# A batched matmul with a subtraction: the first row tile as a segment of its own, and the weight in two contiguous halves

## The chip, the cores and the metric

The kernel runs on one core of one Trainium2 chip. The metric is the device time of one execution, in microseconds (us). Beside it stands a profile of one execution: its span runs from the first to the last instruction, and its device time is a little longer than its span.

## The reference

```python
batch, m, k, n = 16, 512, 1024, 768
def reference(x, weight, sub_value):
    return (np.matmul(x, weight) - sub_value).astype(np.float32)
```

`x` is 16x512x1024, `weight` 1024x768, `sub_value` and the output 16x512x768, all in float32. With the batch flattened this is one matmul of 8192 rows. It reads 33.6 MB of `x`, 3.1 MB of `weight` and 25.2 MB of `sub_value`, and writes 25.2 MB.

## The kernel before, in words

The 8192 rows are cut into 64 row tiles of 128 ("tile 0" to "tile 63"). A tile's work runs through all engines:

1. SyncE (SP) issues the transfers, in the order of the list `TRANSFERS` (L29 to L36). An entry is a kind (x, w, s for `sub_value`, o for output), a first tile and a number of tiles: `('x', 3, 3)` brings tiles 3 to 5 of `x`. A transfer is issued by `issue()` (L243) and waits on SP for what it overwrites or sends: an x transfer for the casts of the tiles whose ring places it takes (16 places, `x_ring`), an s transfer for the outputs that leave the 32 places of `so_ring`, an o transfer for the subtractions. SP does this in order, so a transfer that waits holds up all behind it.
2. ScalarE (ACT) casts a tile to float16 (`cast`, L306, instruction L324). The cast also permutes k, so that pairs of float16 can be transposed as one 32-bit word, and so that a transposed chunk meets the rows of `weight` that sit on the same partitions.
3. TensorE (PE) transposes the tile with four 128x128 matmuls against an identity into PSUM (`transposes`, L342), and ACT copies the result to SBUF (L355, "the evacuation"). For nine pairs of tiles (`ON_DVE`: 10 and 11, 16 and 17, and so on) VectorE (DVE) transposes instead (L375). The casts of these pairs come seven tiles ahead of their use, those of other tiles four ahead.
4. PE multiplies: four chunks c, in each of them two weight loads (L404) and four matmuls of 128x384 (L199), into one of three PSUM accumulators (`po_b`, `NPO = 3`).
5. DVE subtracts (`finish`, L424): it reads the accumulator and the place of `so_ring` that holds `sub_value`, and writes the result in that place. The accumulator is free after that.

Which rows are a tile is set by `SEGMENTS` (L14) and `view` (L127). Rows are grouped in segments of 8 tiles, 1024 rows; in a segment partition p holds 8 consecutive rows, and tile j of the segment takes row j of each partition. So one tile's `x` comes as 128 pieces of 4 KB that lie 32 KB apart in DRAM, and a transfer of n tiles as 128 pieces of n times 4 KB.

The weight is read in the same manner (`w_rows`, L134): partition p holds rows 8p to 8p+7, and each of the two transfers `('w', 0, 2)` and `('w', 2, 2)` takes half of these rows, so 128 pieces of 12 KB, 24 KB apart. DVE casts each half in four instructions (L269).

The head is written out by hand (L445 to L488). `idle(n)` (L433) puts one weight load and n matmuls on zeros into PE's queue, whose result is not used. The first three tiles (`HEAD = 3`) go chunk by chunk, as `weight` arrives in halves. On PE the order is: 14 idle matmuls; transposes of tile 0; 7 idle; tile 0 chunk 0; 1 idle; tile 0 chunk 1; 2 idle; transposes of tiles 1 and 2; 1 idle; chunks 0 and 1 of tiles 1 and 2; chunk 2 of tiles 0, 1, 2; chunk 3 of tiles 0, 1, 2, each followed on DVE by its subtraction; transposes of tiles 3 and 4; tile 3, with the transposes of tile 5 in between. On ACT the casts of tiles 3 and 4 are followed by the evacuations of 3 and 4, then the cast of 5 and its evacuation. From tile 4 on a regular order follows (L492), and from there PE's instructions stand in a loop of six tiles per turn.

The wait that ties PE to the subtractions is in `matmuls`: chunk 0 of a tile takes the accumulator that the tile three before it had, and waits for that tile's `finish` (L397). The one that ties it to ACT is the wait for the tile's evacuation (L393).

Of the kernel before, what the change touches and what calls it, by code (L numbers as in the profile page):

```python
# [8 lines left out]
P = 128  # L9
# [1 line left out]
F32 = mybir.dt.float32  # L11
F16 = mybir.dt.float16

SEGMENTS = [(at, 8) for at in range(0, 64, 8)]  # L14
NX, NSO = 16, 32
N16, NXT, NPT, NPO = 4, 4, 2, 3
N16P, NXTP = 2, 1
# [6 lines left out]
HEAD = 3  # L24
# [2 lines left out]
LOOP = (4, 6, 10)  # L27

TRANSFERS = [  # L29
# [75 lines left out]
def kernel(  # L105
# [7 lines left out]
    nc = tc.nc  # L113
# [10 lines left out]
    n_c = KW // P  # L124
# [6 lines left out]
        rows = flat[first * P : (first + size) * P].rearrange("(p j) c -> p j c", p=P, j=size)  # L131
        return rows[:, at - first : at - first + n]

    w_rows = weight.rearrange("(p k) n -> p k n", p=P)  # L134

    section = ctx.enter_context(ExitStack())
    section.enter_context(tc.tile_critical(no_gpsimd_drain=True))  # L137
# [13 lines left out]
    x_ring = sbuf("x_ring", [P, NX, K], F32)  # L151
# [21 lines left out]
    sp, pe = Queue(nc, nc.sync), Queue(nc, nc.tensor)  # L173
# [69 lines left out]
    def issue():  # L243
        nonlocal known, from_w
        while todo:
            kind, at, n = todo[0]
            span = set(range(at, at + n))
            old = {t - NX if kind == "x" else t - NSO for t in span}
            need, by = {
                "w": (set(), "o"),  # L250
                "x": ({t for t in old if t >= 0}, "cast"),
                "s": ({t for t in old if t >= 0}, "o"),
                "o": (span, "finish"),
            }[kind]
            if not need <= done[by]:
                return
            todo.pop(0)
            done[kind] |= span
            if kind == "w":

                first = NSO - 2 * (n_c - at)
                st = so_ring[:, first : first + 2 * n]
                sem, value = lane((kind, at))
                sp.add(lambda st=st, at=at, n=n: nc.sync.dma_start(out=st, in_=w_rows[:, 2 * at : 2 * (at + n)]), then=(sem, 16))  # L264
                for c in range(at, at + n):
                    for r in range(2):
                        here = so_ring[:, first + 2 * (c - at) + r]
                        dve.add(
                            lambda c=c, r=r, here=here: nc.vector.tensor_copy(out=w_sb[:, c, r], in_=here),  # L269
                            waits=[(sem, value)], then=count("w"),  # L270
                        )
                        staged[first + 2 * (c - at) + r] = so_far["w"]
                    w_at[c] = so_far["w"]
                from_w |= {(("w", at), so_far["w"])}
                continue
            ring, size, flat = {
                "x": (x_ring, NX, x_flat), "s": (so_ring, NSO, sub_flat), "o": (so_ring, NSO, out_flat)
            }[kind]
            here = ring[:, at % size : at % size + n]
            there = view(flat, at, n)  # L280
            waits = []
            if kind == "x" and need:
                waits.append((counter["cast"], max(cast_at[t] for t in need)))
                last = max(need, key=lambda t: cast_at[t])
                known |= {tag for t, tag in of_x.items() if t in cast_at and cast_at[t] <= cast_at[last]}
            if kind == "s":
                for t in need:
                    waits.append(landed["o", t])
                    known.add(of_o[t])
                for t in span:  # L290
                    if t % NSO in staged:
                        waits.append((counter["w"], staged.pop(t % NSO)))
                        known |= {tag for tag, value in from_w if value <= waits[-1][1]}
            if kind == "o":
                waits.append((touched, 16))
                waits.append((counter["finish"], max(finish_at[t] for t in need)))
                known |= {of_s[t] for t in finish_at if finish_at[t] <= max(finish_at[u] for u in need)}
            sem, value = lane((kind, at))
            for t in span:
                landed[kind, t] = (sem, value)  # L300
                {"x": of_x, "s": of_s, "o": of_o}[kind][t] = (kind, at)
            if kind == "o":
                here, there = there, here
            sp.add(lambda here=here, there=there: nc.sync.dma_start(out=here, in_=there), waits, (sem, 16))  # L304

    def cast(mi):  # L306
        assert mi in done["x"]
        done["cast"].add(mi)
        x_in = x_ring[:, mi % NX].rearrange("p (q c r) -> p c q r", c=n_c, r=2)
        first = mi - mi % 2  # L310
        waits = [landed["x", mi]]
        if first in ON_DVE:
            if mi == first:
                b, before = take("x16p", N16P, mi)
                if before is not None:
                    waits.append((counter["pair"], pair_at[before]))
            to = x16p_b[:, slot["x16p", first], mi - first]
        else:
            b, before = take("x16", N16, mi)
            if before is not None:  # L320
                waits.append((counter["turn"], turn_at[before]))
            to = x16_b[:, b]
        to = to.rearrange("p (c q r) -> p c q r", c=n_c, r=2)
        act.add(lambda: nc.scalar.copy(out=to, in_=x_in), waits, count("cast"))  # L324
        cast_at[mi] = so_far["cast"]
        issue()
# [57 lines left out]
    def matmuls(mi, c):  # L384
        first = mi - mi % 2
        on_dve = first in ON_DVE or first == EARLY
        waits = []
        if c == 0:
            b, before = take("po", NPO, mi)
            if on_dve:  # L390
                waits.append((counter["pair"], pair_at[first]))
            if not on_dve:
                waits.append((counter["evac"], evac_at[mi]))  # L393
            elif mi == first:
                waits.append((counter["evac"], evac_at[mi + 1 if mi == EARLY else mi - 1]))
            if before is not None:
                waits.append((counter["finish"], finish_at[before]))  # L397
        if mi < HEAD:
            waits.append((counter["w"], w_at[c]))
        xt = xtp_b[:, slot["xtp", first], mi - first] if on_dve else xt_b[:, slot["xt", mi]]  # L400
        po = po_b[:, slot["po", mi]]
        for r in range(2):
            weights = xt[:, 2 * P * c + r : 2 * P * (c + 1) : 2]
            pe.add(lambda weights=weights: nc.tensor.ldweights(weights, tile_position=(0, 0)), [w for w in waits if w[0] in ready])  # L404
            waits = [w for w in waits if w[0] not in ready]
            for h in range(2):
                last = c == n_c - 1 and r == 1 and h == 1
                pe.add(lambda r=r, h=h, weights=weights: loaded_matmul(
                    po[:, h, :NS],
                    weights,  # L410
                    w_sb[:, c, r, h * NS : (h + 1) * NS],
                    start=(c == 0 and r == 0),
                    stop=(c == n_c - 1 and r == 1),
                ), waits, count("mul") if last else None)
                waits = []
        if c == n_c - 1:
            mul_at[mi] = so_far["mul"]

    def finish(mi):
# [8 lines left out]
        issue()  # L428

    issue()  # L430


    def idle(n):  # L433
        pe.add(lambda: nc.tensor.ldweights(idle_w, tile_position=(0, 0)), [(counter["idle"], 2)])  # L434
        for _ in range(n):
            pe.add(lambda: loaded_matmul(po_b[:, NPO - 1, 0], idle_w, idle_x, start=True, stop=True))
# [4 lines left out]
    def transpose_tile(mi):  # L441
        for f in transposes(mi):
            f()
# [4 lines left out]
    transpose_tile(0)  # L448
    idle(7)
    matmuls(0, 0)  # L450
    idle(1)
    matmuls(0, 1)
    idle(2)
    cast(1)
    cast(2)
    transpose_tile(1)
    transpose_tile(2)
    idle(1)
    for mi in (1, 2):
        for c in (0, 1):  # L460
            matmuls(mi, c)
# [1 line left out]
        matmuls(mi, 2)  # L463
    cast(3)
    cast(HEAD + 1)
    for mi in range(HEAD):
        matmuls(mi, 3)
        finish(mi)
    transpose_tile(3)
    transpose_tile(HEAD + 1)  # L470
    ahead = HEAD + TA
    if EARLY is not None:
        cast(HEAD + 2)
        tr = transposes(HEAD + 2)
        for c in range(n_c):
            matmuls(HEAD, c)
            for f in tr[2 * c : 2 * c + 2] if c < 2 else []:
                f()
        finish(HEAD)
        ahead += 1  # L480
# [84 lines left out]
```

## Time and profile before

| | |
|---|---|
| median of 4 runs | 210.34 us (210.21 to 210.74) |
| the profiled execution's own time | 210.39 us |
| its span | 208.6 us |
| PE, DVE, ACT busy | 196.2, 127.8, 113.4 us |
| bytes moved by DMA | 87.08 MB, mean 417 GB/s |
| first matmul of the loop's kind (L199 on `w_sb`) | starts at 9.49 us |
| last subtraction | 201.52 us, takes 0.96 us |

PE here stands for matmuls and PEld for weight loads, which run beside them. A stage is read from a table by windows: in each stretch of the span it gives the busy time of each engine, the share of the TensorE clock that was granted, the mean busy share of the 16 DMA engines and what they moved. The chain of waits goes back from the last instruction to what released it; it is shown in order of time. DMA shares over 1 in short windows come from packets being counted where they begin.

### The profile page before, as it was taken

The numbers are of one execution on the slowest core, as the hardware profiler recorded it, in microseconds if no ns is written. First come the engines' busy times: TensorE is split into PE (matmuls) and PEld (weight loads), VectorE is DVE, ScalarE is ACT, GpSimd is POOL, SyncE is SP. The second block draws the span as 40 slices with busy tenths as digits, with TensorE's granted clock in tenths as the row PEclk, the third lists the DMA queues.
The fourth block names the chain that finished last, engine by engine and source line by source line (L and its number), as shares of the span: only waits on it lengthen the run. The fifth ranks groups of instructions, "written<-read, shape, count | busy, mean of one in ns | idle before, by whom it ended". The sixth has DMA issues, their size and how long they took to land.

```text
span 208.6 us, 2609 instructions
## 1 busy us (share of the span) xinstructions
PE 196.2 (94%) x1233; PEld 75.5 (36%) x701; DVE 127.8 (61%) x224; ACT 113.4 (54%) x113; POOL 1.0 (0%) x7
## 2 busy tenths in 40 slices
PE   6989699999999999999999999999999999999960
PEld 0133234333434433443442443344344344344310
DVE  2321516955894895597399389469739938942330
ACT  3274688616673761944745676293674747607300
POOL 1000000000000000000000000000000000000000
PEclk9999999999999999999999999999999999999995
DMA  6999999999999899999999999999999999999993
GB/s 216 420 424 434 426 427 434 457 429 401 448 441 459 361 448 448 448 408 421 465 421 427 424 429 434 454 434 413 437 452 393 446 438 424 424 443 434 412 418 127
DMA packets 4932, 87.08 MB, mean 417 GB/s; under 512 B 576, under 2 KB 576, under 8 KB 960
## 3 DMA queue, kind: packets, MB, share of 16 engines
q1 hardware_dynamic: 4896, 87.03, 97.7%
q8 instruction: 1, 0.02, 0.0%
q14 instruction: 3, 0.02, 0.0%
q10 hardware_dynamic: 32, 0.00, 0.0%
HBM read 61.87 MB, written 25.17 MB: 417 GB/s over the span
## 4 chain that ended last, share of the span: by engine, by line
PE 72%; DMA 22%; ACT 2%; issue 1%; DVE 0%; SPq 0%
PE po_b L199 65%; DMA x_ring<-in_x_dram 22%; PE pt_b L342 7%; ACT x_b L324 1%; DVE so_ring L424 0%; ACT xt_b L355 0%; SPq L264 0%; SPq L304 0%; SPq L560 0%; ACT x16p_b L324 0%; SPq L137 0%
## 5 line engine op out<-in xcount | busy, mean ns | idle before, releaser
L199 PE MATMUL po_b<-w_sb,xt_b 128*128 128x384 f16 x704 | 125.8, 326 | 2.5 <-DVE so_ring L424 1.7
L424 DVE TENSOR_TENSOR so_ring<-po_b,so_ring 128x768 f32<-128x768 f32 x64 | 60.6, 956 | 59.9 <-PE po_b L199 44.9
L355 ACT COPY xt_b<-pt_b 128x1024 f16<-128x1024 f16 x44 | 44.5, 1013 | 60.5 <-PE pt_b L342 60.5
L375 DVE STREAM_TRANSPOSE xtp_b<-x16p_b 32x256 f32<-32x256 f32 x144 | 62.7, 435 | 3.6 <-ACT x16p_b L324 1.4
L199 PE MATMUL po_b<-w_sb,xtp_b 128*128 128x384 f16 x320 | 61.4, 326 | 0.2 <-issue 0.2
L404 PEld LDWEIGHTS <-xt_b 128*128 128x128 f16 x352 | 34.4, 98 | 59.8 <-issue 54.2
L324 ACT CAST x_b<-x_ring 128x1024 f16<-128x1024 f32 x46 | 50.7, 1128 | 8.3 <-DMA x_ring<-in_x_dram 8.3
L342 PE MATMUL pt_b<-ident,x_b 128*128 128x128 f32 x184 | 47.5, 274 | 0.9 <-ACT x_b L324 0.7
L342 PEld LDWEIGHTS pt_b<-ident,x_b 128*128 128x128 f32 x184 | 25.2, 141 | 44.8 <-issue 39.1
L324 ACT CAST x16p_b<-x_ring 128x1024 f16<-128x1024 f32 x18 | 20.2, 1124 | 12.2 <-DMA x_ring<-in_x_dram 12.2
L404 PEld LDWEIGHTS <-xtp_b 128*128 128x128 f16 x160 | 15.7, 98 | 18.6 <-issue 16.5
L269 DVE CAST w_sb<-so_ring 128x768 f16<-128x768 f32 x8 | 3.9, 554 | 10.0 <-DMA so_ring<-in_weight_dram 10.0
L199 PE MATMUL po_b<-idle_x,idle_w 128*128 128x512 f16 x25 | 8.5, 488 | 1.7 <-POOL idle_x L179 1.7
L355 ACT COPY xtp_b<-pt_b 128x1024 f16<-128x1024 f16 x2 | 2.0, 1015 | 1.4 <-PE pt_b L342 1.4
L324 ACT ACT_TABLE_LOAD x1 | 1.3, 1283 | 1.5 <-SPq L137 1.5
L434 PEld LDWEIGHTS <-idle_w 128*128 128x128 f16 x5 | 0.5, 98 | 2.1 <-POOL idle_x L179 1.7
L188 DVE TENSOR_TENSOR ident<-along,across 32x32 f32<-32x32 f32 x4 | 0.7, 183 | 0.1
L180 DVE MEMSET ones<- 128x32 f32 x1 | 0.1, 85 | 1.0 <-SPq L137 1.0
L179 POOL MEMSET idle_x<- 128x512 f16 x1 | 0.5, 530 | 0.0
L506 ACT CAST stub<-ident 128x1 f16<-128x1 f32 x2 | 0.4, 205 | 0.0
L185 DVE STREAM_TRANSPOSE across<-along 128x32 f32<-128x32 f32 x1 | 0.2, 211 | 0.0
L483 POOL MEMSET mark<- 128x1 f32 x1 | 0.1, 99 | 24.9 <-ACT xtp_b L355 24.9
(7 smaller groups left out, 1.0 us busy)
## 6 DMA issues: line engine op xcount, KB each, us to landing
so_ring<-in_sub_value_dram SPq DMA_DIRECT2D x7, 3072.0 KB, 24.2
out_dram<-so_ring SPq DMA_DIRECT2D x7, 3072.0 KB, 26.5
x_ring<-in_x_dram SPq DMA_DIRECT2D x5, 4096.0 KB, 23.1
x_ring<-in_x_dram SPq DMA_DIRECT2D x2, 2048.0 KB, 29.4
so_ring<-in_weight_dram SPq DMA_DIRECT2D x2, 1536.0 KB, 9.6
x_ring<-in_x_dram SPq DMA_DIRECT2D x3, 1024.0 KB, 20.7
so_ring<-in_sub_value_dram SPq DMA_DIRECT2D x2, 1536.0 KB, 23.5
x_ring<-in_x_dram SPq DMA_DIRECT2D x1, 3072.0 KB, 27.4
```

Source lines behind the costliest of these rows:

```text
L179: pool.add(lambda: nc.gpsimd.memset(idle_x, 0.0), then=count("idle"))
L188: dve.add(lambda here=here: nc.vector.tensor_tensor(out=ident[here, here], in0=along[here], in1=across[here], op=mybir.AluOpType.is_equal, ...
L199: return nc.tensor.add_instruction(mybir.InstMatmult(name=nc.get_next_instruction_name(), engine=full.engine, ins=list(full.ins), outs=lis ...
L269: lambda c=c, r=r, here=here: nc.vector.tensor_copy(out=w_sb[:, c, r], in_=here),
L324: act.add(lambda: nc.scalar.copy(out=to, in_=x_in), waits, count("cast"))
L342: pe.add(lambda: nc.tensor.transpose(words, from_, ident), waits, count("turn") if last else None)
L355: act.add(lambda: nc.scalar.copy(out=to, in_=pt_b[:, b]), waits, count("evac"))
L375: dve.add(lambda: nc.vector.transpose(xt[b * Q : (b + 1) * Q, :, a * Q : (a + 1) * Q], x16[a * Q : (a + 1) * Q, :, b * Q : (b + 1) * Q],), ...
L404: pe.add(lambda weights=weights: nc.tensor.ldweights(weights, tile_position=(0, 0)), [w for w in waits if w[0] in ready])
L424: dve.add(lambda: nc.vector.tensor_tensor(out=o, in0=po[:, :, :NS], in1=o, op=mybir.AluOpType.subtract), [landed["s", mi], (counter["mul"] ...
L434: pe.add(lambda: nc.tensor.ldweights(idle_w, tile_position=(0, 0)), [(counter["idle"], 2)])
L506: lambda t=t: nc.scalar.copy(out=stub[:, t - n_mt : t - n_mt + 1], in_=ident[:, :1]), [(counter["ident"], made)], count("cast")
```

## The change

Four things are changed.

- Tile 0 becomes a segment of its own, and tiles 1 to 7 one of seven. Tile 0's `x` is then one contiguous stretch of 512 KB (128 pieces of 4 KB that follow each other), and tiles 1 to 7 lie 28 KB apart per partition. Since a transfer can't cross segments, the s transfer of tiles 0 to 3 and the o transfer of tiles 0 to 7 are both cut in two: 36 transfers in place of 34.
- Each half of the weight is contiguous: half g holds rows 512g to 512g+511, partition p the rows 4p to 4p+3 of it. The cast of x reads its tile in the matching order.
- In the head, two of the `idle(1)` are gone. PE does chunk 3 of tile 0 and then the transposes of tile 3, ahead of chunk 3 of tiles 1 and 2.
- On ACT the cast of tile 5 comes ahead of the evacuation of tile 3: casts of tiles 3, 4 and 5, then their evacuations.

From the regular order on, nothing differs but the read pattern of the cast.

```diff
-SEGMENTS = [(at, 8) for at in range(0, 64, 8)]
+SEGMENTS = [(0, 1), (1, 7)] + [(at, 8) for at in range(8, 64, 8)]
...
-    ('x', 0, 1), ('w', 0, 2), ('x', 1, 2), ('w', 2, 2), ('x', 3, 3), ('s', 0, 4),
+    ('x', 0, 1), ('w', 0, 2), ('x', 1, 2), ('w', 2, 2), ('x', 3, 3), ('s', 0, 1), ('s', 1, 3),
...
-    ('x', 24, 8), ('o', 0, 8), ('s', 24, 8), ('x', 32, 8), ('s', 32, 8), ('x', 40, 8),
+    ('x', 24, 8), ('o', 0, 1), ('o', 1, 7), ('s', 24, 8), ('x', 32, 8), ('s', 32, 8), ('x', 40, 8),
...
-    w_rows = weight.rearrange("(p k) n -> p k n", p=P)
+    w_half = weight.rearrange("(g p k) n -> g p k n", g=2, p=P)
...
-in_=w_rows[:, 2 * at : 2 * (at + n)]
+in_=w_half[at // n]
...
-        x_in = x_ring[:, mi % NX].rearrange("p (q c r) -> p c q r", c=n_c, r=2)
+        x_in = x_ring[:, mi % NX].rearrange("p (g q c r) -> p g c q r", g=2, c=2, r=2)
...
-        to = to.rearrange("p (c q r) -> p c q r", c=n_c, r=2)
+        to = to.rearrange("p (g c q r) -> p g c q r", g=2, c=2, r=2)
...
     matmuls(0, 0)
-    idle(1)
     matmuls(0, 1)
...
     transpose_tile(2)
-    idle(1)
     for mi in (1, 2):
...
     cast(3)
     cast(HEAD + 1)
-    for mi in range(HEAD):
+    cast(HEAD + 2)
+    matmuls(0, 3)
+    finish(0)
+    transpose_tile(3)
+    for mi in range(1, HEAD):
         matmuls(mi, 3)
         finish(mi)
-    transpose_tile(3)
     transpose_tile(HEAD + 1)
     ahead = HEAD + TA
     if EARLY is not None:
-        cast(HEAD + 2)
         tr = transposes(HEAD + 2)
```

More of the change, by code (lines that the diff above doesn't have):

```diff
@@ L263, in issue @@
                 sem, value = lane((kind, at))
-                sp.add(lambda st=st, at=at, n=n: nc.sync.dma_start(out=st, in_=w_rows[:, 2 * at : 2 * (at + n)]), then=(sem, 16))
+                sp.add(lambda st=st, at=at, n=n: nc.sync.dma_start(out=st, in_=w_half[at // n]), then=(sem, 16))
                 for c in range(at, at + n):
```

## The prediction, made before the changed kernel was run

> **What bounds the kernel now.** I read the page first, then the table by windows, the chain of waits in order of time, and the timeline of the head. The page:
>
> ```profile
> span 208.6 us, 2609 instructions
> ...
> PE 196.2 (94%) x1233; PEld 75.5 (36%) x701; DVE 127.8 (61%) x224; ACT 113.4 (54%) x113; POOL 1.0 (0%) x7
> ...
> DMA  6999999999999899999999999999999999999993
> ...
> q1 hardware_dynamic: 4896, 87.03, 97.7%
> q8 instruction: 1, 0.02, 0.0%
> q14 instruction: 3, 0.02, 0.0%
> ...
> PE 72%; DMA 22%; ACT 2%; issue 1%; DVE 0%; SPq 0%
> ```
>
> Two things are full at once. PE is busy for 94%, and SP's DMA queue keeps 16 engines busy for 97.7% of the span: 203.8 of 208.6 us. The first packets come at about 2 us and the last end at about 207, so of 205 us of transfers hardly one is idle. So a gain must shorten the transfers; a faster PE alone helps only where PE is what comes late. The windows show where that is:
>
> ```profile
> 20.50:23.20 2.70, 1.00 (x9) 0.86 (x8) 1.00 (x2) 2.10 (x3) 0.00 (x0) 1.00 0.98 410
> ...
> 27.00:51.20 24.20, 23.88 (x154) 9.65 (x89) 14.68 (x25) 14.07 (x15) 0.00 (x0) 1.00 1.00 429
> 51.20:52.20 1.00, 0.86 (x7) 0.16 (x3) 0.28 (x1) 1.00 (x2) 0.00 (x0) 1.00 0.91 393
> 52.20:201.50 149.30, 149.28 (x963) 59.39 (x548) 103.71 (x179) 84.30 (x85) 0.00 (x0) 1.00 1.00 432
> ```
>
> The first figure after the stretch is its length, the second PE's busy time. PE loses 1.70 us at 20.5 to 23.2, some tenths up to 52, and nothing from there to 201.5. The last two figures, DMA share and GB/s, stay at 1 and about 430 throughout. The small loss at 51 matters more than its size, as the chain shows:
>
> ```profile
> 11.98 36.74 DMA x_ring<-in_x_dram
> ...
> 48.77 1.00 issue
> 49.77 0.88 ACT xt_b L355
> ...
> 50.68 1.14 ACT x_b L324
> ...
> 51.86 0.33 PE pt_b L342
> ```
>
> The transfer of x tiles 16 and 17 is issued at 11.98 and lands at 48.7, behind all that is queued ahead of it. ACT waits for it in order (6.33 us idle before the cast at 48.75), and behind that cast stand the evacuation and the cast that PE needs at 50.9 and 51.86. Whatever PE wins before this it waits for here; after it PE has no gap left.
>
> **PE in the head.** This is what the order of the head changes.
>
> ```profile
> 22.20 2.69 DVE L424 TENSOR_TENSOR so_ring<-po_b,so_ring 128x768 f32<-128x768 f32 x3 [5.77 <-DMA so_ring<-in_sub_value_dram]
> ...
> 23.21 0.81 PE L199 MATMUL po_b<-w_sb,xt_b 128*128 128x384 f16 x4 [1.71 <-DVE so_ring L424]
> ```
>
> Tile 3 waits for the accumulator of tile 0, which waits for `sub_value`, all four tiles of which land at 22.2. With tile 0's share alone (0.39 MB, 0.9 us at 430 GB/s, behind x 3 to 5, which land at 18.12), the subtraction of tile 0 can start at about 19.2, when chunk 3 of tile 0 is done. What is late next is the evacuation of tile 3: three casts from 18.12 (1.07 us each in a row) end at 21.3, the evacuation (1.0 us) at 22.3. So tile 3 starts at 22.3 and not at 23.21: 0.9 us. The cast of tile 5 is done by then, so the wait for it inside tile 3 (0.2 us, PE at 24.10) goes as well: tile 4 starts some 1.1 us earlier. The price of the early cast, 1.07 us of ACT ahead of the evacuation of tile 3, is in this sum.
>
> The two removed idle loads and matmuls stood in waits (matmuls at 10.14 and 13.53, 0.38 us each; the real work after them began at 10.43 with the weight cast that ends there, and at 13.95 with the evacuation of tile 1). I cost them at nothing. If PE's clock sank for want of them, PE would slow down before 20 us; the stall of 1.71 us at 21.5 is far longer than the gaps of 0.3 and 0.4 us they leave, and the four matmuls after it keep 0.81 us, as before it.
>
> On the path to the end all this is worth nothing: the 1.1 us become a longer wait at 51, about 1.6 us in place of 0.5, since x 16 and 17 land when the queue has moved what stands ahead.
>
> **The two added transfers.** SP issues one more at 3.35 (0.49 us by the row there) and one more at 55.25 (0.35). Both are covered: the data of s 0 moves at about 18 us, and at 55.25 the queue still has s 16 to 23 to bring, which is 3.1 MB or 7 us of cover. Behind them on SP stand x 6 and 7, which land at 24.5, and s 24 to 31 at 55.90; neither is short. If the cover were gone, each would cost its issue. What they take from the engines: bound below, the last two outputs. The one of 768 KB is issued at 199.90 and takes 6.5 us, the one of 384 KB at 202.50 and takes 4.8, so they land 0.9 us apart, and 0.39 MB at 430 GB/s is 0.9 us: no visible cost. Bound above, the packet records of the trace: a packet of 3,072 B took 121 ns, of 24,576 B 912 ns, so 8 ns are fixed; 8 packets and one semaphore packet (9 ns) more per engine make 0.07 us a transfer, 0.15 us for both. I take +0.1.
>
> The Trainium skill speaks against such cuts: "DMA: Bandwidth & Descriptors", section "Measured (HBM→SBUF, 128 partitions, SWDGE, issued from GpSimd)", wants at least 1 MiB in a transfer, and its section "Anatomy of one DMA — SWDGE (gpsimd) path" gives a fit of about 2.0 us fixed per transfer. Paid on the queue, that would be an estimated +4 us, 214.4. The 0.9 us between the last two outputs say that it is latency which a full queue hides, and the row decides.
>
> **The contiguous layouts.** Bytes and pieces per partition stay (4 KB for x 0, 12 KB for a half of w); only the distance between pieces goes. What there can be to win:
>
> ```profile
> 2.00:4.00 2.00, 2.00 (x6) 0.00 (x0) 0.41 (x3) 0.82 (x1) 0.00 (x0) 1.00 0.92 308
> 4.00:6.00 2.00, 2.00 (x6) 0.00 (x0) 0.00 (x0) 1.11 (x1) 0.00 (x0) 1.00 1.04 414
> 6.00:8.00 2.00, 2.00 (x12) 0.57 (x5) 0.00 (x0) 0.40 (x1) 0.00 (x0) 1.00 0.94 381
> 8.00:10.00 2.00, 1.59 (x9) 0.22 (x3) 1.59 (x4) 0.62 (x1) 0.00 (x0) 1.00 1.03 438
> 10.00:12.00 2.00, 1.67 (x9) 0.37 (x4) 0.38 (x1) 1.16 (x2) 0.00 (x0) 1.00 1.01 430
> ```
>
> From 2 to 8 us the queue moves 2.21 MB, which at the 434 GB/s of the next two rows is 5.1 us: 0.9 us are lost while x 0 and the first half of w move. All of it is the upper bound of the gain, and as it stands at the front of a full queue it would be a gain of the whole. The lower bound: x 1 and 2 and the second half of w move from 8 to 14 us in the same scattered layout at full speed, so distance alone costs nothing, and the 0.9 us are a start that any layout has; the gain is 0. A loss has no row: no transfer here became slower by smaller distance. I take 0.2, nearer to the full-speed rows. The cast reads the same number of elements, 8 bytes out of 16 in place of 8 out of 32; ACT's 1.12 us a cast against 113.4 us in all leave room, and 0 is taken.
>
> **Sum.** 210.39 (the profiled execution) + 0.1 - 0.2 + 0 for PE = **210.3 us**; the profiled execution stands 0.05 above the median of the four runs, which I leave in.
>
> **Rivals.**
>
> *The start gets all of its 0.9 us.* If scattered pieces are what slows the first two transfers, the queue shifts by up to 0.9, and PE can follow, as it then has 1.6 us in hand at 51. 210.39 + 0.1 - 0.9 = 209.6. For it: only the first transfers are slow. Against it: the scattered ones right after them are not.
>
> *PE's gain passes to the end.* If the landing at 48.7 did not hold ACT, the 1.1 us would come through: 210.39 + 0.1 - 0.2 - 1.1 = 209.2. For it: PE is 72% of the chain. Against it: the chain's wait of 36.74 us, and a queue that is full to 204.
>
> *One more instruction fetch: slower.* The end is not set by the mean engine:
>
> ```profile
> 203.00:204.00 1.00, 0.00 (x0) 0.00 (x0) 0.00 (x0) 0.00 (x0) 0.00 (x0) 1.00 0.96 396
> 204.00:205.00 1.00, 0.00 (x0) 0.00 (x0) 0.00 (x0) 0.00 (x0) 0.00 (x0) 0.63 0.76 307
> 205.00:206.00 1.00, 0.00 (x0) 0.00 (x0) 0.00 (x0) 0.00 (x0) 0.00 (x0) 0.50 0.19 77
> 206.00:207.00 1.00, 0.00 (x0) 0.00 (x0) 0.00 (x0) 0.00 (x0) 0.00 (x0) 0.50 0.10 40
> ```
>
> From 205 to 207 only two or three of 16 engines still work (0.19 and 0.10 of 16). Every transfer is spread over all of them, so these engines had other work or were slowed. The page's instruction queues are such work: in the packet records one packet of 16 KB took 0.94 us and three of 8 KB 0.31 us each. SP's program grows by two transfers and a wait, DVE's by a wait, and PE's shrinks by four instructions. If one program crosses into another block, and the block is fetched by the engine that is last anyway, the end moves by 0.3 to 0.9 us: 210.6 to 211.2, say 211.0. It decides as soon as a fifth packet shows in the instruction queues on a late engine; a fetch on any other engine is free, as these are done 2 us earlier.
>
> **Chances.** A measurement of this kernel can tell about 0.2%, 0.42 us, from no change: below 209.9 is faster, above 210.8 slower. The forecast, its own range 209.9 to 210.8: 0.66. The start's 0.9 us: 0.13. PE's gain: 0.05. The fetch: 0.16. Faster 0.18, same 0.66, slower 0.16. The range reaches down to the start's case, 209.5, and up into the fetch case, 210.9; it leaves out PE's gain and most of the fetch case.
>
> **What would show it.** PE's first matmul of tile 3 near 22.3 and not 23.21, tile 4 near 25.8; the subtraction of tile 0 near 19.2; the chain of waits still through a transfer of x tiles into ACT at 48 to 49 us, and a longer PE gap at 50 to 52; the queue's share still near 97%, with 5,184 packets (36 transfers of 144 on q1). The layouts: GB/s from 2 to 8 us, against 2.21 MB moved. I would be wrong if PE ended before 200.8, if the queue ran empty before the last outputs, or if the landing of x 16 and 17 moved by more than 0.4 us.

## The result, and the profile after

The changed kernel takes 210.76 us (median of 41 runs, 210.39 to 211.44), the kernel before 210.40 us in the same comparison (63 runs). The ratio is 1.0017, 95% interval 1.0013 to 1.0021: **0.36 us slower**, where 0.1 us faster was forecast. The time lies in the range that the prediction gives, but the change went the other way, and its interval is clear of 1. One run of the kernel before took 734.66 us; the ratio compares fast runs alone and leaves it out. The profiled execution took 211.02 us, 0.26 above its median, so 0.36 of the 0.63 us between the two profiled executions is the change.

The page of the changed kernel, the lines that answer to those shown of before:

```profile
span 209.2 us, 2609 instructions
...
DMA  6999999999999999999999999999999999999992
...
q1 hardware_dynamic: 5184, 87.03, 97.6%
q8 instruction: 1, 0.02, 0.0%
q14 instruction: 3, 0.02, 0.0%
...
PE 47%; DMA 44%; ACT 4%; DVE 1%; issue 1%; SPq 1%; DVEq 0%; ACTq 0%
```

The packets are the 5,184 that 36 transfers should have, the queue is as full as before, and the instruction queues have the same four packets: the extra fetch of the slower rival did not come. The chain now goes through DMA for 44%.

The head did what the walk in the prediction said. Timeline of the changed kernel (start, length):

```profile
19.12 0.96 DVE L424 TENSOR_TENSOR so_ring<-po_b,so_ring 128x768 f32<-128x768 f32 x1 [2.91 <-PE po_b L199]
...
22.04 0.83 PE L199 MATMUL po_b<-w_sb,xt_b 128*128 128x384 f16 x4 [0.58 <-ACT xt_b L355]
...
25.43 0.81 PE L199 MATMUL po_b<-w_sb,xtp_b 128*128 128x384 f16 x4 [0.18 <-issue]
```

and tile 4 in the kernel before:

```profile
26.89 0.81 PE L199 MATMUL po_b<-w_sb,xtp_b 128*128 128x384 f16 x4 [0.18 <-issue]
```

The subtraction of tile 0 starts at 19.12 (forecast 19.2), tile 3 at 22.04 (22.3; 23.21 before), now released by ACT's evacuation and not by DVE, and tile 4 at 25.43 (25.8; 26.89 before). PE was 1.46 us ahead; 0.22 us of this it owes to x tiles 3 to 5, which landed that much sooner (17.88 us, 18.10 before). By 52 us all but 0.17 us of it was gone, by the table by windows:

```profile
27.00:51.20 24.20, 22.83 (x147) 9.05 (x83) 14.14 (x24) 12.74 (x14) 0.00 (x0) 1.00 1.02 435
51.20:52.20 1.00, 0.87 (x7) 0.26 (x3) 0.12 (x1) 1.00 (x2) 0.00 (x0) 1.00 1.12 467
52.20:201.50 149.30, 149.19 (x962) 59.30 (x547) 103.55 (x179) 84.11 (x85) 0.00 (x0) 1.00 1.00 429
```

PE idles 1.37 us between 27 and 51.2 (0.32 before). The chain in order of time shows the same wait in the same place; x 16 and 17 land at 48.56, 0.17 us sooner than before:

```profile
11.75 36.81 DMA x_ring<-in_x_dram
48.60 1.00 issue
49.60 0.89 ACT xt_b L355
50.51 1.15 ACT x_b L324
...
140.53 30.77 DMA out_dram<-so_ring
171.31 14.70 DMA so_ring<-in_sub_value_dram
186.10 0.97 DVE so_ring L424
```

The last three pieces are new in the chain: an output that lands at 171.31 lets SP send the last `sub_value`, and PE waits for its subtraction. Up to tile 58 PE keeps its lead of 0.17 us; tile 59, at 187.11, starts 0.10 later than before. The last subtraction starts at 201.62, 0.10 later too.

So far the forecast held, and so did the gain of the layouts: from 2 to 8 us the queue moved 2.31 MB, 0.10 MB or 0.24 us more than before (I had taken 0.2). One pair of executions gives only a rough size: over all profiled executions of this document it is 2.29 to 2.36 MB with the weight in halves (8 executions) and 2.07 to 2.25 without (12), on average 0.18 MB or 0.41 us at 434 GB/s.

```profile
2.00:4.00 2.00, 2.00 (x6) 0.00 (x0) 0.40 (x3) 0.83 (x1) 0.00 (x0) 1.00 0.99 353
4.00:6.00 2.00, 2.00 (x6) 0.00 (x0) 0.00 (x0) 1.10 (x1) 0.00 (x0) 1.00 1.01 406
6.00:8.00 2.00, 2.00 (x11) 0.57 (x5) 0.00 (x0) 0.15 (x1) 0.00 (x0) 1.00 0.95 397
```

What failed came at 70 us. The table by windows there, the kernel before:

```profile
69.00:70.00 1.00, 1.00 (x8) 0.47 (x4) 1.00 (x2) 1.00 (x2) 0.00 (x0) 1.00 1.17 426
70.00:71.00 1.00, 1.00 (x9) 0.44 (x5) 0.96 (x4) 0.90 (x1) 0.00 (x0) 1.00 0.40 131
71.00:72.00 1.00, 1.00 (x9) 0.43 (x4) 0.97 (x3) 0.09 (x1) 0.00 (x0) 1.00 0.89 377
```

and the changed kernel:

```profile
69.00:70.00 1.00, 1.00 (x9) 0.51 (x5) 0.99 (x3) 1.00 (x2) 0.00 (x0) 1.00 1.81 524
70.00:71.00 1.00, 1.00 (x9) 0.43 (x4) 0.97 (x3) 0.74 (x1) 0.00 (x0) 1.00 0.11 33
71.00:72.00 1.00, 1.00 (x9) 0.36 (x4) 0.97 (x3) 0.26 (x1) 0.00 (x0) 1.00 0.57 227
```

Packets count where they begin, so a share of 1.81 followed by 0.11 means that long packets began together and few new ones could start: in 70 to 72 us 0.26 MB began, against 0.51 MB before. In the packet records these are the last packets of x 24 to 31, the transfer ahead of the first output. A packet of 32 KB usually takes 1.21 us; of the 128 of this transfer 22 took 1.36 to 1.93 us (12 took 1.39 to 1.62 before), and one of the engine that is last took 2.84 us (2.10 before). I call this the dip. The lead of the queue, that is how much sooner it is done with the same transfer, did not survive it. A transfer raises its semaphore 16 times, once for each engine; the first and the last of these events show the first and the last engine. The first engine was done with x 16 and 17 0.28 us sooner than before (46.77 against 47.05), with x 24 to 31 only 0.10 sooner (71.39 against 71.49); the last engine was done with x 24 to 31 0.56 later (74.29 against 73.73) and with the last output 0.65 later (207.94 against 207.29). The end of the changed kernel:

```profile
204.00:205.00 1.00, 0.00 (x0) 0.00 (x0) 0.00 (x0) 0.00 (x0) 0.00 (x0) 0.88 0.90 366
205.00:206.00 1.00, 0.00 (x0) 0.00 (x0) 0.00 (x0) 0.00 (x0) 0.00 (x0) 0.50 0.22 89
206.00:207.00 1.00, 0.00 (x0) 0.00 (x0) 0.00 (x0) 0.00 (x0) 0.00 (x0) 0.50 0.11 43
207.00:209.20 2.20, 0.00 (x0) 0.00 (x0) 0.00 (x0) 0.00 (x0) 0.00 (x0) 0.50 0.02 7
```

Again two to four engines work on alone after 205, and now to almost 208.

### The profile page after: what moved, and what is told of

Read it like the earlier page. It is cut to its first block, busy times and chain, and to the rows that moved or that the text cites. A ratio compares the mean times of both kernels' runs of the same rounds, so it can differ in the third digit from the quotient of the medians.

```text
span 209.2 us, 2609 instructions
## 1 busy us (share of the span) xinstructions
PE 196.4 (94%) x1231; PEld 75.4 (36%) x699; DVE 127.7 (61%) x224; ACT 113.2 (54%) x113; POOL 1.0 (0%) x7
## 3 DMA queue, kind: packets, MB, share of 16 engines
q1 hardware_dynamic: 5184, 87.03, 97.6%
## 4 chain that ended last, share of the span: by engine, by line
PE 47%; DMA 44%; ACT 4%; DVE 1%; issue 1%; SPq 1%; DVEq 0%; ACTq 0%
PE po_b L199 42%; DMA x_ring<-in_x_dram 22%; DMA out_dram<-so_ring 15%; DMA so_ring<-in_sub_value_dram 7%; PE pt_b L342 5%; ACT x_b L324 2%; ACT xt_b L355 1%; DVE so_ring L424 1%; ACT x16p_b L324 0%; SPq L304 0%; SPq L264 0%; SPq L560 0%; DVEq L58 0%; ACTq L58 0%; SPq L137 0%
## 5 line engine op out<-in xcount | busy, mean ns | idle before, releaser
L199 PE MATMUL po_b<-idle_x,idle_w 128*128 128x512 f16 x23 | 8.0, 510 | 1.7 <-POOL idle_x L179 1.7
```

What stands on the lines that cost most here:

```text
L199: return nc.tensor.add_instruction(mybir.InstMatmult(name=nc.get_next_instruction_name(), engine=full.engine, ins=list(full.ins), outs=lis ...
```

## The experiments

Two questions: what makes the dip, and which part of the change costs the time. The letters of the theories are those of the expectations. Ratios are to the kernel before on the same chip, with 95% intervals; 0.001 is 0.21 us.

**The cuts and the weight, one by one.** The first theory (A) was that a short first output makes the dip.

```diff
e1, to the kernel before:  -('o', 0, 8),   +('o', 0, 1), ('o', 1, 7),
e2, to the kernel before:  -('s', 0, 4),   +('s', 0, 1), ('s', 1, 3),
e3, to the changed one:    -('o', 0, 1), ('o', 1, 7),   +('o', 1, 7), ('o', 0, 1),
e4, to the kernel before:  w_half and the cast's pattern of the changed one, nothing else
```

e1: 

> The kernel before with the output of tiles 0 to 7 cut into tile 0 and tiles 1 to 7, nothing else changed. Theory A (a short first write to the output makes all engines wait once at about 70 us): 0.3 to 0.6 us slower than before, and in the stretch 70 to 72 us fewer bytes begin than the 131 and 377 GB/s of before (33 and 227 in the changed kernel). Theory B (every added transfer costs about the same, in packets): 0.07 to 0.2 us slower, 70 to 72 as before. Theory C (the 28 KB pitch or the weight's layout costs): no change.

e2: 

> The kernel before with the sub_value of tiles 0 to 3 cut into tile 0 and tiles 1 to 3, nothing else changed. Theory A: 0 to 0.1 us slower (packets alone), since no write is touched. Theory B: the same 0.07 to 0.2 us as for the cut of the output. Theory C: no change. All: tile 3 starts earlier on PE, at about 22.2, and the gain is gone at 52 us.

e3: 

> The changed kernel with the two outputs in the other order: tiles 1 to 7 first, then tile 0. Theory A: the long transfer takes the first write, so the time falls back by 0.3 to 0.6 us to within 0.15 us of before, and 70 to 72 us look like before. Theory B and theory C: as the changed kernel, 0.3 to 0.4 us over before.

e4: 

> The kernel before with the weight in two contiguous halves and the cast to match, nothing else changed. Theory A and B: no change or up to 0.2 us faster, if the first half lands earlier than 8.4 us. Theory C: 0.2 to 0.4 us slower, with less than 431 GB/s in some stretch after 8 us or casts longer than 1.13 us.

Measured: e1 1.0004 (0.9995 to 1.0012), e2 1.0004 (0.9995 to 1.0013), e3 1.0025 (1.0016 to 1.0033), e4 1.0013 (1.0004 to 1.0022). A falls: the cut output alone costs nothing that shows, and with the long output first the changed kernel stays slow. B's 0.07 to 0.2 us can't be told from nothing here. The weight's halves alone are slower, by some 0.27 us, as C had it, but not by C's mechanism: apart from 67 to 75 us (388 GB/s, 417 before) the queue is as fast as before (432 GB/s from 8 to 67 us and 433 from 75 to 200; 433 and 431 before), and a cast takes 1.13 us as before. e4 moved more in its first 8 us (382 GB/s from 2 to 8 us, 368 before), and had the dip.

**Where the dip stands.**

```diff
e5, to the kernel before:  -('x', 24, 8), ('o', 0, 8), ('s', 24, 8),   +('x', 24, 8), ('s', 24, 8), ('o', 0, 8),
e8, to the kernel before:  +('s', 24, 8), ('x', 24, 8), ('o', 0, 8),
e6, to the changed one:    the small transfer at the start touches 128 rows of the output in place of 16
e7, to the kernel before:  that small transfer and the wait for it left out
e9, to the changed one:    s 24 to 31 between x 24 to 31 and the outputs, as in e5
e10, to the changed one:   s 24 to 31 ahead of x 24 to 31, as in e8
```

e5: 

> The kernel before with sub_value of tiles 24 to 31 sent ahead of the output of tiles 0 to 7, so that the first output comes one transfer (7.3 us) later. All profiles so far show slow packets of all engines at 68 to 71.6 us, on the last packets of x tiles 24 to 31, just ahead of the first output. Theory D (the first output causes it): the dip in GB/s moves to about 76 to 79 us. Theory E (it stands at a time) and theory F (it belongs to x 24 to 31): the dip stays at 70 to 72 us. Time: within 0.2 us of before by all three.

e6: 

> The changed kernel with 128 in place of 16 rows of the output touched by the small transfer at the start (128 bytes each, sent by ACT; they are overwritten later). Theory D, in the form that the first output pays for memory that was not touched before: the dip at 70 to 72 us goes (over 400 GB/s in each of the two), and the kernel falls to 0.3 to 0.6 us below the changed one. Theories E and F: the dip stays and the time is that of the changed kernel, or up to 0.2 us more for the 112 more small packets.

e7: 

> The kernel before without the small transfer at the start that touches 16 rows of the output (and without the wait for it). Theory D: the dip ahead of the first output gets deeper or new dips come at later outputs, 0.5 us slower or more. Theories E and F: dip and time as before, within 0.2 us.

e8: 

> The kernel before with sub_value of tiles 24 to 31 sent ahead of x of tiles 24 to 31, a look at where the dip is; x lands 7.3 us later, so PE may wait and the time is not compared. Theory E: the dip stays at 68 to 72 us, now in the packets of sub_value. Theories D and F: it moves to about 76 to 79 us, the end of x 24 to 31, which still stands just ahead of the first output.

e9: 

> The changed kernel with sub_value of tiles 24 to 31 ahead of the outputs of tiles 0 to 7. The same move on the kernel before took the dip away, but its head had lost 1.2 us by chance. Here the head is early again. Theory G as a time: the dip stays at 68 to 72 us. Theory D (the first output): no dip there, one at 76 to 79 us, or none at all; if none, the time falls by 0.3 us or more from the changed kernel.

e10: 

> The changed kernel with sub_value of tiles 24 to 31 ahead of x of tiles 24 to 31. Theory G as a time: slow packets at 68 to 72 us, in whatever is moving then, and a time as the changed kernel. Theories D and F: slow packets at 76 to 79 us, at the end of x 24 to 31. PE's casts of tiles 24 on have 7 us less to spare; if PE waits for them, the last subtraction moves later than 201.6 us by that wait.

Measured: e5 1.0005 (0.9996 to 1.0015), e6 1.0029 (1.0019 to 1.0039), e7 0.9997 (0.9988 to 1.0007), e8 one run of 210.40 us, e9 1.0027 (1.0016 to 1.0037), e10 1.0039 (1.0025 to 1.0052; its last subtraction is at 203.67, so PE did wait for the late x). In e5 and e8 there is no dip to speak of, at either place, which no theory had said; their heads had moved little. In e9 and e10 the head is early and the dip is there, and it has moved. e9, then e10, by windows:

```profile
70.00:72.00 2.00, 2.00 (x15) 0.92 (x9) 1.93 (x6) 0.99 (x2) 0.00 (x0) 1.00 0.88 377
76.00:78.00 2.00, 2.00 (x15) 0.59 (x6) 1.94 (x4) 2.00 (x4) 0.00 (x0) 1.00 1.19 393
```

```profile
70.00:72.00 2.00, 2.00 (x15) 0.92 (x9) 1.93 (x6) 0.99 (x2) 0.00 (x0) 1.00 0.87 377
76.00:78.00 2.00, 2.00 (x15) 0.59 (x6) 1.94 (x4) 0.00 (x1) 0.00 (x0) 1.00 0.97 295
```

At 70 to 72 us packets run at their usual time, and packets that begin from 75.5 to 78.5 us are slow on all engines: in e9 the last packets of `sub_value` 24 to 31 (24 KB, 1.03 to 1.86 us in place of 0.91), in e10 the last ones of x 24 to 31. So the dip is tied neither to a time (E, and G read as a time) nor to x 24 to 31 (F), but to the read transfer ahead of the first output, as D says. Nothing speaks for the price of untouched memory: e6 touches eight times as many rows and keeps the dip, e7 touches none and is as fast as before. (Most of the output stays untouched in both, so this form of D is not excluded in full.)

**The lead and the dip.** Two sums from the packet records say more than the single runs: the time that packets took over the usual time of their size, as a mean of the 16 engines, in the first 9 us (the loss in the head) and from 66 to 79.5 us, where the first output's turn comes (the dip). e11, which moves other bytes, is left out.

```text
                 head  dip                    head  dip
before           0.63  0.29   e4 (halves)     0.52  0.62
e1               0.86  0.16   changed         0.51  0.72
e2               1.00  0.08   e17 (changed)   0.48  0.51
e5               1.20  0.00   e3 (halves)     0.39  0.81
e7               0.79  0.17   e6 (halves)     0.43  0.63
e8               1.00  0.02   e9 (halves)     0.42  0.64
e12              0.87  0.16   e10 (halves)    0.45  0.68
e13              0.99  0.08
e14              0.65  0.33
e15              0.90  0.11
e16 (before)     0.92  0.15
e18              0.60  0.46
```

The right column has the weight in halves, the left one has not. The two sums add up to 0.92 to 1.24 us in all 19 profiled executions; their correlation is -0.95, and the slope is -1.04. Taken over all, what the head gains is given back ahead of the first output, one for one. Within the left column alone the slope is -0.70, and the right one spans too little to tell (correlation -0.42), so "one for one" is a rough rule. The semaphore events say the same without a usual time. The first engine is done with x 16 and 17 at 46.66 to 46.88 us where the weight is in halves and at 46.89 to 47.44 where it is not. With x 24 to 31 it is done at 71.32 to 71.75 and at 71.30 to 71.71, so the lead is gone (e11 is left out of both, and of the second e5, e8, e9 and e10, in which that transfer does not stand in its place ahead of the output). e18 shows that the layout is not needed for it: old weight, an early head in that execution, a large dip.

**One transfer more.** Theory G made a wall of this: the stretch of reading can't be over before a certain point, so a delay in the head should be free.

```diff
e11, to the changed one, in issue(), ahead of ('x', 8, 4); the first cast into x16p_b waits for it:
+            if (kind, at) == ("x", 8):
+                there = x16p_b.bitcast(F32).rearrange("p a b k -> p (a b k)")[:, :512]
+                sp.add(lambda there=there: nc.sync.dma_start(out=there, in_=x_flat[:P, :512]), then=(spare, 16))
e12, e18, to the changed one: weight and cast as in the kernel before
```

e11: 

> The changed kernel with one more transfer in the head, 256 KB of x into a buffer that no one reads (0.6 us of the queue), ahead of x tiles 8 to 11. Theory G (a wall: the queue can't have finished x 24 to 31 before about 71.4 us; what the head wins before is lost there, and the engine that is last pays double): the dip at 68 to 72 us shrinks to that of before or less, and the kernel is no slower than the changed one, 0 to 0.4 us faster, though it moves more. Theory H (the queue is simply full, each byte counts): 0.6 us slower than the changed kernel, 0.9 to 1.0 over before.

e12: 

> The changed kernel with the weight and the cast as before; the segment of tile 0, the cuts and the order of the head stay. Theory G: it depends on the lead at 61 us alone: if the first 8 us move fewer bytes than in the changed kernel, the dip is smaller and the kernel is within 0.2 us of before. Theory H: 0.1 to 0.2 us over before, for the two transfers. If it stays 0.3 us or more over before, the weight is not what costs.

Measured: e11 1.0049 (1.0036 to 1.0063), e12 1.0022 (1.0012 to 1.0031). The dip of e11 did shrink, to 0.20 us, but the kernel became 1.03 us slower than before, 0.67 more than the changed one, and 256 KB are 0.61 us at 430 GB/s. The 0.67 us are a difference of two comparisons; next to e9, measured in the same one, e11 is 0.45 us slower. The time went with H: the queue is full, and each byte counts. G as a wall that makes a delay free falls. For the cancelling of lead and dip e11 is no support: its two sums add up to some 0.7 us, outside the range above, and its profile is of one of its two fastest executions (210.75 us, the six go from 210.73 to 211.64).

**The other parts.**

```diff
e13, to the kernel before: SEGMENTS of the changed one and both cuts
e14, to the kernel before: the head's order of the changed one
e15, to the kernel before: both cuts
e16: the kernel before;  e17: the changed kernel
```

e13: 

> The kernel before with tile 0 as a segment of its own and both cuts that this forces; weight, cast and the order of the head as before. Theory H (each transfer and packet on a full queue counts, the layout gives nothing): 0.15 us over before, as e15. Theory I (the segment of tile 0 costs: its pieces or the 28 KB pitch): 0.3 to 0.5 us over before, 0.2 or more over e15. Theory J (the order of the head costs): as e15.

e14: 

> The kernel before with the order of the head of the changed one alone: two idle matmuls less, chunk 3 of tile 0 and the transposes of tile 3 forward, the cast of tile 5 forward. Theories H and I: within 0.1 us of before. Theory J: 0.2 us or more over before.

e15: 

> The kernel before with both cuts alone, 36 transfers. Theory H: 0.15 us over before by the packet records, up to 0.3 if the engine that is last pays more. Theories I and J: 0.1 to 0.2 us over before.

e16: 

> The kernel before, unchanged, under another name: all theories expect a ratio of 1 within its interval. If it stands 0.1 us or more above, that much of every ratio here belongs to the comparison.

e17: 

> The changed kernel once more, as the partner of the next run. All theories: 0.3 to 0.45 us over before, with slow packets of all engines at 68 to 72 us, on the last packets of x 24 to 31.

e18: 

> The changed kernel with the weight and the cast as before, once more. Theory K (the weight's halves carry it: they bring the first half of the weight sooner, the whole queue leads, and the transfer ahead of the first output is slowed by more than the lead): within 0.15 us of before, fewer bytes moved from 4 to 8 us than in the changed kernel, a small dip at 70 to 72 us. Theory L (the other parts together): 0.3 us or more over before, as the changed kernel.

Measured: e13 1.0000 (0.9989 to 1.0011), e14 0.9996 (0.9988 to 1.0005), e15 0.9995 (0.9985 to 1.0006), e16 0.9997 (0.9987 to 1.0006), e17 1.0014 (1.0005 to 1.0023), e18 1.0005 (0.9996 to 1.0014). I and J fall: neither the segment nor the order of the head costs anything that shows. The comparison on this chip, on which e13 to e18 ran, is not biased (e16). That the order wins nothing is not shown by e14: without the cut of `sub_value` PE still waits for it there. The first matmul of tile 3 in e14, then in e18, which has order and cut:

```profile
23.41 0.81 PE L199 MATMUL po_b<-w_sb,xt_b 128*128 128x384 f16 x4 [1.21 <-DVE so_ring L424]
```

```profile
22.12 0.83 PE L199 MATMUL po_b<-w_sb,xt_b 128*128 128x384 f16 x4 [0.58 <-ACT xt_b L355]
```

In e18 PE is at tile 4 at 25.48 us, 1.41 sooner than before, and the kernel is not faster.

What remains is K, the weight's halves. The kernels that have them and are otherwise comparable stand at 1.0013 to 1.0029 (the changed one, e3, e4, e6, e9, e17), every interval clear of 1. Those without stand at 0.9995 to 1.0005 (e1, e2, e5, e7, e13, e14, e15, e16, e18), every interval with 1 inside, except e12, whose runs went from 210.10 to 211.29. e12 and e18 are one kernel with nearly the same median (210.63 and 210.65 us); what differs is the kernel before on the two chips (210.16 and 210.40). e17 and e18 on one chip differ by less than their intervals, and the 23 runs of e12 and e18 together have a mean ratio of 1.0014, as e17 has (1.0015). So K rests on the whole set, above all on e4, and not on taking the halves out of the changed kernel. L, that the other parts cost something together though none does alone, is not excluded.

None of these kernels is faster than the kernel before beyond its interval; the lowest ratio is e15's.

## Why the prediction went wrong

Point by point, by its own steps:

- **What bounds it: right.** A full queue. e11 measures it: 256 KB more cost 0.67 us over the changed kernel, 0.45 over e9 in the same comparison.
- **PE in the head: right,** with its place. 1.46 us won by tile 4 (1.1 forecast), waited for again at x 16 and 17. e18, with 1.41 us won by tile 4 and the old weight, is at 1.0005.
- **The two cuts: not contradicted.** +0.1 taken; e15 gives -0.1 with an interval of -0.3 to +0.1. The 2 us per transfer that the Trainium skill's "DMA: Bandwidth & Descriptors" gives in the section "Anatomy of one DMA — SWDGE (gpsimd) path", as a fit to transfers of another path, are not paid on a full queue here; for two transfers they would be an estimated 4 us.
- **The layouts: the step that failed.** The size of the gain in the head was right in the first pair of profiles (0.24 us for 0.2); 0.4 is nearer to the average. Wrong was the sentence "as it stands at the front of a full queue it would be a gain of the whole". I carried the lead to the end without looking at a stretch in which the queue is slow for another reason, though the profile of before shows one, in the slices and in the windows at 70 to 71 us (131 GB/s). The prediction read a DMA share of 1 and about 430 GB/s "throughout" off windows of up to 149 us, in whose means a dip of 2 us does not show. There the lead was given back, and more: the halves alone came to +0.27 us (e4) in place of -0.2. "A loss has no row" put at nothing what then happened; its reason, that no transfer became slower by smaller distance, holds for the packets and not for the end.
- **The rivals.** The start's 0.9 us stopped at 0.24 (0.4 on average), PE's gain did not pass, the fetch did not come. The slower rival had the right place, the engine that is last, and the wrong cause.

That lead and dip cancel gives 0; the 0.3 us beyond show at the last engine. In the six profiled executions with halves named under K the first engine is done with the last output at 205.03 us on average, the last one at 207.71. In the eleven without halves (all but e8, where the last subtraction is 1.0 us late) it is 205.05 and 207.39. The engines that are first end together; the last one ends 0.32 us later, which is about the measured difference. The single executions overlap (207.36 to 208.02 us with halves, 207.01 to 207.81 without). The step is at the dip: the slowest packet ahead of the first output took 2.47 to 2.93 us in the five of the six where it is one of 32 KB, and in the eleven at most 2.11, but for 2.55 in e18. In the changed kernel it ends at 72.80 us, the latest of the packets over 1.3 us, and the last engine lands its part of that transfer some one packet later, at 74.29. The dip alone does not tell the time of an execution: e15 took 210.91 us with a dip of 0.11, e3 210.60 with 0.81.

**What stays open.** Why the reads ahead of the first output slow down, and why by as much as the queue is ahead. Not a time, not the transfer, not its neighbour's length: these were tried. Touching more or fewer rows of the output beforehand changed nothing. Whether the first output's own reads and writes are at work while x still moves can't be seen in records that give a packet's begin and length. That the last engine loses more than the others there is seen; why is not. The link from the halves to an earlier head holds in all 20 profiled executions, by a small margin over e18 (2.29 MB against 2.25). Whether the halves are the whole cost stays open: e12 is left without a cause, and the other parts together were measured only there and in e18.

## What to carry to other kernels

When a queue is full from start to end, a gain at its front is a gain only if every later stretch keeps it: look for slow stretches in the profile before the sum is made, and price the lead at nothing until it has passed the last of them. The end is set by the engine that is last and not by the mean: look at the windows after the last instruction, where a share of 0.1 is one or two engines. And a change of 0.2% needs each part measured by itself with the old kernel once more beside it; four parts of this one measured nothing beyond 0.2 us, and measuring each alone does not say what they do together.

## What the runs showed of the hardware

- Lead and dip nearly cancel: in 19 profiled executions the time lost in the first 9 us and the time lost ahead of the first output add up to 0.92 to 1.24 us. The first engine's lead at 47 us (46.66 to 46.88 against 46.89 to 47.44) is gone at 71 us (71.32 to 71.75 against 71.30 to 71.71).
- An instruction fetch costs a DMA engine more than its own packet: behind the packet of 16 KB (0.94 us) and of 8 KB (0.31 us) the next data packet took 0.24 to 0.53 us longer, in the kernel before 0.50 us and 0.53, 0.24 and 0.53 us. So a fetch kept its engine for 1.4 us and for 0.55 to 0.84 us.
- A packet's time is 8 ns and its bytes at 27 bytes per ns (121 ns for 3 KB, 912 for 24 KB, 1,213 for 32 KB), and the same for the second half of the weight 24 KB apart and contiguous (460 ns for 12 KB), after the first 9 us and outside the dip and the fetches.
